# A decoder trunk on one core: 1/rms multiplied into the results of the up products instead of their operands

## The chip, the cores and the metric

The kernel runs on one core of one Trainium2 chip. The metric is the device time of one execution in microseconds (us). The profile tells the engines apart as PE (TensorE matmul), PEld (TensorE weight load), DVE (VectorE), ACT (ScalarE), POOL (GpSimd) and SP (SyncE, which here issues the transfers).

## The reference

One inference step of a two-layer trunk on 1024 prompt tokens and 8 x 4 sample tokens (1056 columns in the kernel, D = 1024). Layer 0 is a gated linear recurrence, layer 1 a dilated window attention. Each ends with the same MLP of width 4096, and the change is about that:

```python
def _rmsnorm(x, gain):
    return x * lax.rsqrt(jnp.mean(x * x, axis=-1, keepdims=True) + EPS) * gain

def _sqrelu_mlp(x, w_up, w_down):
    return jnp.square(jax.nn.relu(x @ w_up)) @ w_down

x = x + h
x = x + _sqrelu_mlp(_rmsnorm(x, mlp_norm[layer]), mlp_w_up[layer], mlp_w_down[layer])
```

## The kernel before, in words

All activations are kept transposed: 128 feature rows by token columns, eight row blocks `xr[:, k, :]`. In the MLPs and in the output products ahead of them the 1056 columns are cut in three chunks, 384, 384 and 288 (`MLPCH`). Every large fp32 product is made of three matmuls of rounded halves: high by high, low by high and high by low (`mm3`, L185 to L187, and `mmx`, L805 to L807). So every operand is split in two: ACT copies it into the rounded type (the H half), and another engine subtracts that copy from it (the L half).

**Weights.** `_prep` loads a weight in two transfers (`wraw`, issued on SP), splits it (`whi` on ACT, L131; `wlo` on POOL, L132), and for a down weight `w_dn` also makes four sums (L159 to L161 on DVE, L162 on POOL) and splits these into `whix` (ACT) and `wlox` (POOL). The sums belong to a scheme in the manner of Strassen, by which four products of 2 x 2 blocks are made with seven. The raw tiles lie in two buffers, so a transfer can start only when POOL has finished the `wlo` of the tile that it replaces.

**Norm.** `norm` (L254) runs as a lane, a generator that is advanced one step between products. Per chunk it squares each row block (ACT, L263 and L266), adds the squares up (DVE, L267) and sums over the 128 rows with one matmul against a constant matrix (PE, L273). ACT then makes 1/rms by logarithm and exponential (L239, L240). For each row block DVE multiplies x by gain and 1/rms (L281), ACT copies the high half (L232), and POOL (five of eight) or DVE (three) subtracts for the low half (L233).

**MLP.** `mlp` takes the 32 hidden blocks in eight groups of four. For a group it makes the up product j = 0, then four down products (`down`) of the group before, and then the up products j = 1 to 3. An up product has 24 matmuls per chunk and leaves a PSUM tile `pj`, of which there are four. `ev_up` empties it: ACT takes the relu out of PSUM (L720), DVE squares it (L721), and the result, or differences of results (L726, L743), is split (ACT L709; L710 on DVE or POOL). `down` works on PSUM tiles A, B and C; DVE adds each partial result to the residual (`add`, L819), and the next product into the same tile waits for that add. The third chunk goes through `alone` and `resid` (L211).

The order of instructions on each engine comes from a scheduler that goes by program order and priorities (`high_priority`). Each engine then runs its own instructions strictly in that order.

Of the kernel before, what the change touches and what calls it, by code (L numbers as in the profile page):

```python
# [10 lines left out]
F32 = mybir.dt.float32  # L11
F32R = mybir.dt.float32r
U8 = mybir.dt.uint8
AF = mybir.ActivationFunctionType
# [4 lines left out]
P = 128  # L19
KD = 8  # L20
# [26 lines left out]
class Kern:  # L47
# [202 lines left out]
    def norm(self, gi, ops, need, gaps=(3, 3, 2), hp=0):  # L250
# [3 lines left out]
        for c, sl in enumerate(self.chunks_of(ops)):  # L254
# [16 lines left out]
            with self.tc.high_priority(offset=hp):  # L271
# [3 lines left out]
                for k in range(KD):  # L275
# [5 lines left out]
                        nc.vector.scalar_tensor_tensor(t, xk, self.gains[:, gi, k:k + 1], r, op0=ALU.mult, op1=ALU.mult)  # L281
                    self.split(c, k, ops, t, pool=(k % 3 != 0))

    def chunks_of(self, ops):
        return CHUNKS if ops[0][0].shape[-1] == CW else MLPCH


    def phase_a(self):
# [140 lines left out]
        part(range(4, 8))  # L429
        ctx.close()  # L430
        self.open_norm()
        self.lanes.append(self.norm(G_M0, ops, NEED, (3, 3, 0), 100))
        ctx = ExitStack()
        self.wx = ctx.enter_context(tc.tile_pool(name="wxA", bufs=4, reuse_waits="tile"))
        self.rawx = True
# [264 lines left out]
    def mlp(self, layer, ops, after=None):  # L700
# [11 lines left out]
        def ev_up(hs, hb, j, tmp, last):  # L712
# [3 lines left out]
            def ev(c, ps):  # L716
                n = ps.shape[-1]
                with tc.high_priority(offset=200):
                    r = self.tmp(n)
                    nc.scalar.activation(r, ps, AF.Relu)  # L720
                nc.vector.tensor_tensor(r, r, r, op=ALU.mult)  # L721
                if c == 2:
                    return split(hs[2 * e + i], r, True)
                tmp[e, c] = r

                sub = lambda x, y: nc.vector.tensor_tensor(x, y, x, op=ALU.subtract)  # L726
                h = hb[i]
                if c == 0:
                    split(h[e], r, True)
                elif last:  # L730
                    split(h[2 + e], r)
                elif e == 0:
                    t = tmp[0, 0]
                    sub(t, r)
                    split(h[3], t)
                else:
                    split(h[2], r)
                    t2, t3, t4 = tmp[0, 0], tmp[0, 1], tmp[1, 0]
                    sub(t3, r)
                    split(h[5], t3)  # L740
                    sub(t2, r)
                    split(h[4], t2)
                    nc.vector.tensor_tensor(t4, t4, t2, op=ALU.subtract)  # L743
                    split(h[6], t4)
# [30 lines left out]
        for g in range(NG + 1):  # L775
# [9 lines left out]
                        self.down(2 * p, self.wnext(), hs, hb)  # L785
            if g < NG:
                ups(g, range(1, GS))
        w = [self.wnext() for _ in range(4)]
        if after:
            self.lanes.append(self.norm(None, after, NEED))  # L790
# [69 lines left out]
    def phase_c(self, ops):  # L860
# [51 lines left out]
        while not self.merged:  # L912
            self.tick()
        w = [self.wnext() for _ in range(4)]
        self.lanes.append(self.norm(G_M1, ops, NEED))
        for c, sl in enumerate(MLPCH):
            while self.merged < -(-min(sl.stop, NP_ + P) // P) * 2 - (c == 2):
                next(self.queue[0])
            for m, t, ks in self.quarter_items(w, 4):
# [1 line left out]
                self.mm3(ps, t, ops[c], ks)  # L921
                self.resid(m, c, ps)
                self.tick()
        self.drain()
        cxa.close()
        self.open_norm()
        return ops
# [542 lines left out]
```

## Time and profile before

| | |
|---|---|
| time, median of 3 runs (lowest, highest) | 3043.11 us (3035.6, 3047.07) |
| time of the profiled execution | 3045.13 us |
| its span, from first to last instruction | 3043.4 us |
| mean granted TensorE clock | 0.989 |
| busy PE, PEld | 2875.0 (94%), 2757.8 us (91%) |
| busy DVE, ACT, POOL | 1796.0 (59%), 1282.9 (42%), 1338.3 us (44%) |

The busy share says how long an engine worked, not whether anyone waited for it. The MLPs take the stretches from about 765 to 1440 us and 2320 to 2990 us of the span; the stretches from 660 and from 2262 us are the output products ahead of them, with the norm that they overlap. A row of the timeline gives start and duration of an operation and, in brackets, how long the engine had stood idle before it and what released it. PEclk is the share of full TensorE speed that the chip granted.

### The profile page before, as it was taken

The page shows a single profiled execution, that of the slowest core. Times are in us where ns is not written, and L with a number is a line of the kernel's source. Part 1 is how long each engine was busy: PE and PEld are TensorE (multiplying, and loading weights), DVE is VectorE, ACT ScalarE, POOL GpSimd, SP SyncE. Part 2 cuts the span into 40 slices and gives each one's busy share as a digit, 9 for nine tenths or more (in the row PEclk, how much of TensorE's full clock was granted, in tenths as well). Part 3 has the DMA queues.
Part 4 walks back from the last instruction along what each step waited for, and adds up shares of the span by engine and source line. Part 5 has one row for each costly group of instructions (what it writes and reads, how often), then busy time and mean ns, then how long its engine had stood idle before and what let it go on. Part 6 is the DMA issues. An engine that isn't in the chain of part 4 may idle for free.

```text
span 3043.4 us, 47407 instructions
## 1 busy us (share of the span) xinstructions
PE 2875.0 (94%) x18144; PEld 2757.8 (91%) x18144; DVE 1796.0 (59%) x3467; ACT 1282.9 (42%) x2972; POOL 1338.3 (44%) x1149
## 2 busy tenths in 40 slices
PE   6998999889999999999899999999999999999999
PEld 5888888889999999999899889889888999999999
DVE  8777777876544455543654565665676455544442
ACT  6555656643332222332445544555544223332221
POOL 5444444453544444544463553333225445444442
PEclk9999999999999999999999999999999999999999
DMA  3100211230111111112212233332641111111112
GB/s 113 36 30 30 71 40 29 69 123 18 46 49 43 49 46 46 49 43 63 84 62 68 84 99 108 124 117 71 195 150 42 44 48 49 42 46 46 49 49 86
DMA packets 131956, 201.92 MB, mean 66 GB/s; under 512 B 26320, under 2 KB 65872, under 8 KB 129680
## 3 DMA queue, kind: packets, MB, share of 16 engines
q1 hardware_dynamic: 131728, 198.88, 20.9%
q8 instruction: 143, 2.34, 0.3%
q14 instruction: 85, 0.70, 0.1%
HBM read 164.04 MB, written 34.80 MB: 65 GB/s over the span
## 4 chain that ended last, share of the span: by engine, by line
PE 56%; DVE 10%; POOL 8%; issue 7%; DMA 5%; ACT 3%; POOLq 0%; SPq 0%; DVEq 0%; ACTq 0%
PE pj L185 10%; PE pj L186 10%; PE pj L187 10%; POOL wlo L132 4%; PE pj L805 4%; PE pj L806 4%; PE pj L807 4%; DMA wraw<-w_dn 3%; PE g L806 2%; PE g L805 2%; PE g L807 2%; POOL wlox L132 2%; PE g L1143 2%; PE g L1115 1%; PE g L1130 1%
## 5 line engine op out<-in xcount | busy, mean ns | idle before, releaser
L185 PE MATMUL pj<-opH,whi 128*128 128x352 f32 (+2 forms) x3408 | 1136.7, 334 | 9.9 <-DVE xr L211 3.5
L186 PE MATMUL pj<-opL,whi 128*128 128x352 f32 (+2 forms) x3408 | 1110.1, 326 | 5.0 <-POOL opL L233 3.2
L187 PE MATMUL pj<-opH,wlo 128*128 128x352 f32 (+2 forms) x3408 | 1107.0, 325 | 2.9 <-POOL wlo L132 2.7
L132 POOL TENSOR_TENSOR wlo<-wraw,whi 128x512 fp32r<-128x512 f32 x404 | 546.5, 1371 | 913.1 <-ACT whi L131 882.1
L185 PEld LDWEIGHTS pj<-opH,whi 128*128 128x128 f32 x3408 | 645.8, 190 | 30.6 <-issue 16.9
L186 PEld LDWEIGHTS pj<-opL,whi 128*128 128x128 f32 x3408 | 646.7, 190 | 17.9 <-POOL opL L233 6.6
L187 PEld LDWEIGHTS pj<-opH,wlo 128*128 128x128 f32 x3408 | 645.6, 189 | 6.9 <-POOL wlo L132 4.1
L131 ACT ACTIVATE whi<-wraw 128x512 fp32r<-128x512 f32 x404 | 232.6, 621 | 546.6 <-PE g L806 439.9
L721 DVE TENSOR_TENSOR tmp<-tmp 128x384 f32<-128x384 f32 (+1 forms) x192 | 169.5, 883 | 311.2 <-ACT tmp L720 311.2
L819 DVE TENSOR_TENSOR xr<-xr,pj 128x384 f32<-128x384 f32 x336 | 183.7, 553 | 138.5 <-PE pj L807 138.3
L496 POOL TENSOR_TENSOR lv<-b 128x512 f32<-128x512 f32 x112 | 125.0, 1127 | 102.7 <-PE g L593 58.4
L720 ACT ACTIVATE tmp<-pj 128x384 f32<-128x384 f32 (+1 forms) x192 | 86.9, 453 | 189.3 <-PE pj L187 188.5
L132 POOL TENSOR_TENSOR wlox<-wsum,whix 128x512 fp32r<-128x512 f32 x112 | 151.0, 1368 | 0.6 <-ACT whix L131 0.6
L162 POOL TENSOR_TENSOR wsum<-wraw,wsum 128x256 f32<-128x256 f32 x56 | 43.7, 781 | 168.0 <-DVE wsum L160 153.8
L1117 DVE CUSTOM_DVE_ANT_0 pr<-g,band,rq 128x128 f32<-128x128 f32 (+1 forms) x192 | 67.9, 405 | 79.9 <-PE g L1115 76.3
L1120 ACT ACTIVATE pr<-pr,nm 128x128 f32<-128x128 f32 (+1 forms) x192 | 84.1, 440 | 68.0 <-DVE nm L1118 67.8
L148 POOL TENSOR_TENSOR wraw<-wraw,gains 128x512 f32<-128x512 f32 x72 | 91.4, 1275 | 40.0 <-DMA wraw<-w_q 33.3
L211 DVE TENSOR_TENSOR xr<-xr,pj 128x384 f32<-128x384 f32 (+1 forms) x132 | 67.2, 516 | 69.7 <-PE pj L187 37.5
L709 ACT ACTIVATE hbH<-tmp 128x384 fp32r<-128x384 f32 x106 | 54.9, 526 | 121.2 <-DVE tmp L721 72.8
L967 POOL TENSOR_TENSOR q<-q,cos 32x512 f32<-32x512 f32 x48 | 89.8, 1877 | 30.2 <-DVE rsw L966 28.9
L159 DVE TENSOR_TENSOR wsum<-wraw 128x256 f32<-128x256 f32 x56 | 23.8, 425 | 131.5 <-DMA wraw<-w_dn 131.3
L806 PE MATMUL g<-hL,whi 128*128 128x288 f32 x336 | 100.5, 299 | 0.0
(399 smaller groups left out, 5917.8 us busy)
## 6 DMA issues: line engine op xcount, KB each, us to landing
wraw<-w_up SPq DMA_DIRECT2D x128, 256.0 KB, 2.8
wraw<-w_dn SPq DMA_DIRECT2D x128, 256.0 KB, 2.8
wraw<-w_in SPq DMA_DIRECT2D x64, 256.0 KB, 2.8
wraw<-w_q SPq DMA_DIRECT2D x48, 256.0 KB, 2.9
ub<-us SPq DMA_DIRECT2D x32, 256.0 KB, 2.2
cc<-ck SPq DMA_DIRECT2D x8, 1024.0 KB, 5.1
cc<-cv SPq DMA_DIRECT2D x8, 1024.0 KB, 5.4
wraw<-w_kv SPq DMA_DIRECT2D x24, 256.0 KB, 2.9
```

Source lines behind the costliest of these rows:

```text
L131: nc.scalar.activation(hi[:, j:j + 4, :], raw, AF.Copy)
L132: nc.gpsimd.tensor_tensor(lo[:, j:j + 4, :], raw, hi[:, j:j + 4, :].bitcast(F32), op=ALU.subtract)
L148: nc.gpsimd.tensor_tensor(raw, raw, self.gains[:, gi, j:j + 4][:, :, None].to_broadcast([P, 4, P]), op=ALU.mult)
L185: nc.tensor.matmul(ps, wh[:, kw, :], xh[:, kx, :], start=(i == 0), stop=False)
L186: nc.tensor.matmul(ps, wh[:, kw, :], xl[:, kx, :], start=False, stop=False)
L187: nc.tensor.matmul(ps, wl[:, kw, :], xh[:, kx, :], start=False, stop=(i == len(ks) - 1))
L496: nc.gpsimd.tensor_tensor(r(lv), r(b), r(b)[:, :, h - 1:h].to_broadcast([P, 256 // h, 2 * h]), op=ALU.subtract)
L721: nc.vector.tensor_tensor(r, r, r, op=ALU.mult)
L805: nc.tensor.matmul(ps, wh[:, kw, :], xh, start=start and i == 0, stop=False, skip_group_check=True)
L806: nc.tensor.matmul(ps, wh[:, kw, :], xl, start=False, stop=False, skip_group_check=True)
L807: nc.tensor.matmul(ps, wl[:, kw, :], xh, start=False, stop=stop and i == len(items) - 1, skip_group_check=True)
L819: self.nc.vector.tensor_tensor(x(i, c), x(i, c), ps, op=ALU.add)
```

## The change

`norm_late` takes the place of `norm` in the two MLPs. Its operands are the split of x times gain, without 1/rms: ACT makes the high half in one operation, DVE the low half (multiply and subtract in one), and POOL none. 1/rms goes to tiles of its own, one per chunk (`scale`, with a number behind the name in the order of instructions). `ev_up` multiplies it in: DVE takes the maximum with zero and multiplies by the scale, straight from PSUM, and ACT squares. The entry of the second MLP no longer runs all lanes to their end before it goes on.

```diff
--- before.py
+++ after.py
@@ -280,6 +280,44 @@
                     else:
                         nc.vector.scalar_tensor_tensor(t, xk, self.gains[:, gi, k:k + 1], r, op0=ALU.mult, op1=ALU.mult)
                     self.split(c, k, ops, t, pool=(k % 3 != 0))
+
+    def open_scales(self):
+
+        self.sctx = ExitStack()
+        p = self.sctx.enter_context(self.tc.tile_pool(name=f"sc{self.wi}", bufs=1, side="right", reuse_waits="tile"))
+        self.scale = [p.tile([P, sl.stop - sl.start], F32, name=f"scale{c}") for c, sl in enumerate(MLPCH)]
+
+    def norm_late(self, gi, ops, need, gaps=(3, 3, 2), hp=0):
+
+        nc = self.nc
+        steps = 0
+        for c, sl in enumerate(MLPCH):
+            n, r = sl.stop - sl.start, self.scale[c]
+            for k in range(KD):
+                while steps < need[c] - (KD - 1 - k):
+                    yield
+                    steps += 1
+                with self.tc.high_priority(offset=hp):
+                    if k == 0:
+                        nc.scalar.activation(r, self.xr[:, 0, sl], AF.Square)
+                    else:
+                        t = self.sq(n)
+                        nc.scalar.activation(t, self.xr[:, k, sl], AF.Square)
+                        nc.vector.tensor_tensor(r, r, t, op=ALU.add)
+            with self.tc.high_priority(offset=hp + 60):
+                for k in range(KD):
+                    h, l = (t[:, k, :] for t in ops[c])
+                    x, g = self.xr[:, k, sl], self.gains[:, gi, k:k + 1]
+                    nc.scalar.activation(h, x, AF.Copy, scale=g)
+                    nc.vector.scalar_tensor_tensor(l, x, g, h.bitcast(F32), op0=ALU.mult, op1=ALU.subtract)
+            for _ in range(gaps[c]):
+                yield
+                steps += 1
+            with self.tc.high_priority(offset=hp):
+                ps = self.bank()[:, :n]
+                nc.tensor.matmul(ps, self.onesD, r, start=True, stop=True)
+                nc.scalar.activation(r, ps, AF.Ln, bias=self.eps[:, 0:1])
+                nc.scalar.activation(r, r, AF.Exp, scale=-0.5)
 
     def chunks_of(self, ops):
         return CHUNKS if ops[0][0].shape[-1] == CW else MLPCH
@@ -429,7 +467,9 @@
         part(range(4, 8))
         ctx.close()
         self.open_norm()
-        self.lanes.append(self.norm(G_M0, ops, NEED, (3, 3, 0), 100))
+        self.open_scales()
+        self.lanes.append(self.norm_late(G_M0, ops, NEED, hp=100))
+        next(self.lanes[-1])
         ctx = ExitStack()
         self.wx = ctx.enter_context(tc.tile_pool(name="wxA", bufs=4, reuse_waits="tile"))
         self.rawx = True
@@ -717,8 +757,8 @@
                 n = ps.shape[-1]
                 with tc.high_priority(offset=200):
                     r = self.tmp(n)
-                    nc.scalar.activation(r, ps, AF.Relu)
-                nc.vector.tensor_tensor(r, r, r, op=ALU.mult)
+                    nc.vector.scalar_tensor_tensor(r, ps, 0.0, self.scale[c], op0=ALU.max, op1=ALU.mult)
+                nc.scalar.activation(r, r, AF.Square)
                 if c == 2:
                     return split(hs[2 * e + i], r, True)
                 tmp[e, c] = r
@@ -785,6 +825,7 @@
                         self.down(2 * p, self.wnext(), hs, hb)
             if g < NG:
                 ups(g, range(1, GS))
+        self.sctx.close()
         w = [self.wnext() for _ in range(4)]
         if after:
             self.lanes.append(self.norm(None, after, NEED))
@@ -912,7 +953,9 @@
         while not self.merged:
             self.tick()
         w = [self.wnext() for _ in range(4)]
-        self.lanes.append(self.norm(G_M1, ops, NEED))
+        self.open_scales()
+        self.lanes.append(self.norm_late(G_M1, ops, NEED))
+        next(self.lanes[-1])
         for c, sl in enumerate(MLPCH):
             while self.merged < -(-min(sl.stop, NP_ + P) // P) * 2 - (c == 2):
                 next(self.queue[0])
@@ -921,7 +964,9 @@
                 self.mm3(ps, t, ops[c], ks)
                 self.resid(m, c, ps)
                 self.tick()
-        self.drain()
+        while self.queue:
+            if next(self.queue[0], "end") == "end":
+                self.queue.popleft()
         cxa.close()
         self.open_norm()
         return ops
```

The order of instructions moves with it. On DVE, around the first down product of a group (a middle group of the first MLP; `pj` and `g` are PSUM tiles, `xr` the residual, `wsum` the sums of the down weight, `hpL` the low half of a hidden block), the row before reads

```order
L159 TENSOR_TENSOR wsum<-wraw 128x256
L721 TENSOR_TENSOR tmp<-tmp 128x384
L160 TENSOR_TENSOR wsum<-wsum,wraw 128x256
L161 TENSOR_TENSOR wsum<-wraw 128x256
L721 TENSOR_TENSOR tmp<-tmp 128x384
L726 TENSOR_TENSOR tmp<-tmp 128x384
L710 TENSOR_TENSOR hpL<-tmp,hpH 128x384
L819 TENSOR_TENSOR xr<-xr,pj 128x384
L721 TENSOR_TENSOR tmp<-tmp 128x288
L819 TENSOR_TENSOR xr<-xr,g 128x384
L819 TENSOR_TENSOR xr<-xr,pj 128x384 x2
```

and now

```order
L760 SCALAR_TENSOR_TENSOR tmp<-pj,scale_6842 128x384
L159 TENSOR_TENSOR wsum<-wraw 128x256
L161 TENSOR_TENSOR wsum<-wraw 128x256
L160 TENSOR_TENSOR wsum<-wsum,wraw 128x256
L760 SCALAR_TENSOR_TENSOR tmp<-pj,scale_6843 128x384
L766 TENSOR_TENSOR tmp<-tmp 128x384
L750 TENSOR_TENSOR hpL<-tmp,hpH 128x384
L760 SCALAR_TENSOR_TENSOR tmp<-pj,scale_6844 128x288
L860 TENSOR_TENSOR xr<-xr,pj 128x384
L860 TENSOR_TENSOR xr<-xr,g 128x384
L860 TENSOR_TENSOR xr<-xr,pj 128x384 x2
```

The squares that stood on DVE (L721) are gone from the row; in their places stand the new operations that read PSUM (L760). The one of the third chunk (288 columns), which stood behind the first add, now stands ahead of it, and the second chunk's weight sums (L160, L161) no longer wait behind the first chunk's square.

On ACT, at the same place (`whix` and `whi` are the weights' high halves, `hpH` and `h0H` those of hidden blocks), before:

```order
L720 ACTIVATE tmp<-pj 128x384
L709 ACTIVATE hpH<-tmp 128x384
L131 ACTIVATE whix<-wsum 128x512 x2
L720 ACTIVATE tmp<-pj 128x384
L709 ACTIVATE hpH<-tmp 128x384
L131 ACTIVATE whi<-wraw 128x512 x2
L720 ACTIVATE tmp<-pj 128x288
L709 ACTIVATE h0H<-tmp 128x288
```

and now:

```order
L761 ACTIVATE tmp<-tmp 128x384
L749 ACTIVATE hpH<-tmp 128x384
L131 ACTIVATE whix<-wsum 128x512 x2
L761 ACTIVATE tmp<-tmp 128x384
L749 ACTIVATE hpH<-tmp 128x384
L131 ACTIVATE whi<-wraw 128x512 x2
L761 ACTIVATE tmp<-tmp 128x288
L749 ACTIVATE h0H<-tmp 128x288
```

Every relu (L720) has become a square (L761) at the same place in the row; it reads a tile that DVE wrote instead of PSUM.

On DVE at the entry of the second MLP, where the third chunk's squares are summed for the last norm matmul (`us` before, a `scale` tile now; `pt` is a working tile), before:

```order
L281 SCALAR_TENSOR_TENSOR pt<-xr,gains,rstd 128x384 x3
L267 TENSOR_TENSOR us<-us,pt 128x288
L211 TENSOR_TENSOR xr<-xr,pj 128x288 x3
L267 TENSOR_TENSOR us<-us,pt 128x288
L233 TENSOR_TENSOR opL<-pt,opH 128x384
L267 TENSOR_TENSOR us<-us,pt 128x288 x5
L281 SCALAR_TENSOR_TENSOR pt<-xr,gains,rstd 128x288 x3
```

and now:

```order
L211 TENSOR_TENSOR xr<-xr,pj 128x288
L312 SCALAR_TENSOR_TENSOR opL<-xr,gains,opH 128x288 x2
L211 TENSOR_TENSOR xr<-xr,pj 128x288
L312 SCALAR_TENSOR_TENSOR opL<-xr,gains,opH 128x288 x2
L306 TENSOR_TENSOR scale_21786<-scale_21786,pt 128x288 x2
L760 SCALAR_TENSOR_TENSOR tmp<-pj,scale_21784 128x384
L760 SCALAR_TENSOR_TENSOR tmp<-pj,scale_21785 128x384
```

Before, the second chunk's last scale operations (L281) and five of the seven sums (L267) stood in a block around the last residual adds (L211). Now the third chunk's own scale operations (L312) stand there, and only two sums are left behind the last residual add. On PE the matmul that uses the sum moves 17 matmuls down the row, to just ahead of the third chunk of the first up product.

## Rows read from the trace of the kernel before

**Rows 1.** Busy time by window (start:end, length; PE, PEld, DVE, ACT, POOL; PEclk; DMA; GB/s).

```profile
660.00:765.00 105.00, 101.60 (x605) 97.63 (x604) 63.66 (x99) 41.66 (x87) 42.45 (x34) 1.00 0.17 55
...
765.00:1440.00 675.00, 655.95 (x4051) 652.00 (x4050) 328.68 (x554) 201.90 (x402) 313.77 (x266) 0.99 0.16 48
...
2262.00:2320.00 58.00, 50.85 (x296) 47.80 (x296) 47.12 (x82) 29.79 (x66) 26.02 (x22) 0.94 0.09 29
...
2320.00:2990.00 670.00, 652.57 (x4030) 648.93 (x4030) 329.98 (x556) 200.69 (x399) 311.08 (x264) 0.99 0.15 47
...
906.00:910.00 4.00, 3.52 (x11) 3.53 (x12) 1.34 (x3) 1.15 (x2) 3.41 (x3) 0.58 0.30 91
...
2306.00:2310.00 4.00, 4.00 (x14) 3.79 (x13) 2.13 (x5) 2.25 (x5) 0.63 (x1) 0.56 0.00 0
```

**Rows 2.** Waits of PE, whole program (us in total, times, longest).

```profile
PE pj L805 <- DVE xr L819: 36.5, 26, 1.9
```

**Rows 3.** Timeline of PE (start, us, what, [idle before <- releaser]).

```profile
992.19 0.45 PE L805 MATMUL pj<-hqH,whix 128*128 128x384 f32 x1 [1.68 <-DVE xr L819]
...
999.93 0.44 PE L805 MATMUL pj<-hqH,whix 128*128 128x384 f32 x1 [1.16 <-DVE xr L819]
```

**Rows 4.** Timeline of DVE, 980 to 1002 us.

```profile
984.50 0.55 DVE L721 TENSOR_TENSOR tmp<-tmp 128x384 f32<-128x384 f32 x1
...
985.30 0.42 DVE L161 TENSOR_TENSOR wsum<-wraw 128x256 f32<-128x256 f32 x1
...
987.39 1.56 DVE L721 TENSOR_TENSOR tmp<-tmp 128x384 f32<-128x384 f32 x1 [1.67 <-ACT tmp L720]
...
989.06 1.46 DVE L726 TENSOR_TENSOR tmp<-tmp 128x384 f32<-128x384 f32 x1
...
991.11 0.56 DVE L710 TENSOR_TENSOR hpL<-tmp,hpH 128x384 fp32r<-128x384 f32 x1 [0.59 <-ACT hpH L709]
...
991.59 0.55 DVE L819 TENSOR_TENSOR xr<-xr,pj 128x384 f32<-128x384 f32 x1
...
997.48 0.43 DVE L159 TENSOR_TENSOR wsum<-wraw 128x256 f32<-128x256 f32 x1 [2.81 <-DMA wraw<-w_dn]
...
998.86 1.01 DVE L819 TENSOR_TENSOR xr<-xr,pj 128x384 f32<-128x384 f32 x2
```

**Rows 5.** Timeline of ACT, the same stretch.

```profile
986.35 0.64 ACT L131 ACTIVATE whix<-wsum 128x512 fp32r<-128x512 f32 x1 [0.22 <-POOL wsum L162]
...
986.89 0.47 ACT L720 ACTIVATE tmp<-pj 128x384 f32<-128x384 f32 x1
...
990.56 0.52 ACT L709 ACTIVATE hpH<-tmp 128x384 fp32r<-128x384 f32 x1 [3.20 <-DVE tmp L726]
...
990.99 1.13 ACT L131 ACTIVATE whi<-wraw 128x512 fp32r<-128x512 f32 x2
```

**Rows 6.** Timeline of POOL, the same stretch.

```profile
987.26 2.85 POOL L132 TENSOR_TENSOR wlox<-wsum,whix 128x512 fp32r<-128x512 f32 x2
...
991.68 2.76 POOL L132 TENSOR_TENSOR wlo<-wraw,whi 128x512 fp32r<-128x512 f32 x2 [1.57 <-ACT whi L131]
```

**Rows 7.** Chain of waits, 955 to 1003 us (start, us, what).

```profile
978.59 2.97 POOL wlo L132 x2
...
981.57 2.49 DMA wraw<-w_dn
```

**Rows 8.** Groups of one shape, DVE (count | busy us, mean ns | idle before).

```profile
L819 DVE TENSOR_TENSOR xr<-xr,pj 128x384 f32<-128x384 f32 x336 | 183.7, 553 | 138.5 <-PE pj L807 138.3
...
L993 DVE SCALAR_TENSOR_TENSOR kt<-pj,hg,rstd 128x352 f32<-128x352 f32 x12 | 9.1, 760 | 18.5 <-ACT rstd L240 18.5
...
L281 DVE SCALAR_TENSOR_TENSOR tmp<-xr,gains,rstd 128x384 f32<-128x384 f32 x16 | 16.4, 1071 | 0.4 <-ACT rstd L240 0.4
```

**Rows 9.** Waits of PE at the entries: 700 to 765, then 2275 to 2320 us.

```profile
PE pj L185 <- DVE xr L211: 2.5, 1, 2.5
...
PE g L273 <- DVE us L267: 4.1, 2, 3.7
```

## The prediction

> **What bounds the kernel now.** I read five views: the busy table with its windows by stage, the waits of TensorE, the timelines of the vector engines around one wait, the chain of waits, and the groups of instructions by shape. TensorE (PE) is busy in 2875.0 of 3043.4 us, so what can be won is the time in which it stands still, or runs at the lower clock. The change touches only the two MLPs and their entries. There PE is busy 655.95 of 675 us and 652.57 of 670 us in the steady part, and 101.60 of 105 and 50.85 of 58 us at the entries [rows 1]. It does not remove a matmul, so the whole prize is bounded by the idle time of these four windows, 19.05 + 17.43 + 3.40 + 7.15 = 47.0 us, and the time lost to a lower granted clock in them.
>
> In the steady part there is one wait only: the first matmul of a down product waits for the add that empties its PSUM tile, 26 times, 36.5 us in all [rows 2]. That is the idle time of the two steady windows, 19.05 + 17.43, to the last tenth, 13 waits in each. The waits come in pairs, two per group of four hidden blocks; the pair at 992.19 (1.68 us) and 999.93 (1.16 us) [rows 3] is the usual one.
>
> Why is the add late? Read the four vector queues together. PE finished the tile long before, but the add (991.59) stands in VectorE's (DVE) queue behind work for the next group's first up product: a square (987.39, 1.56 us), a difference (989.06, 1.46 us), and a subtraction (991.11, 0.56 us) that itself waited for ScalarE's (ACT) copy [rows 4, 5]. That sequence starts when ACT is through with whix (986.35 + 0.64 = 986.99) and reads the relu out of PSUM. Durations add up without a gap: 0.47 relu + 1.56 square + 1.46 difference + 0.52 copy + 0.56 subtraction + 0.55 add = 5.12, from 986.99 to 992.11; the add ended at 992.14. The second wait is the same lateness passed on through the weights: the copy's end (990.99) lets whi start, then GpSimd's (POOL) wlo (991.68, 2.76 us), then the next weight's transfer, which lands before DVE's wsum at 997.48, which stands ahead of the adds at 998.86 [rows 4 to 6]. The square and the difference take 1.46 to 1.56 us because POOL's wlox runs from 987.26 to 990.11 [rows 6]; the same operation took 0.55 us at 984.50, before POOL began.
>
> **The change part by part.**
>
> *Evacuation of the up products.* Relu on ACT and square on DVE become a maximum-and-scale on DVE that reads PSUM, and a square on ACT. On the path of the first wait this takes out 0.47 + 1.56 us and puts in ACT's square. ACT's operations on 384 columns take 0.47 to 0.52 us [rows 5]; I take 0.53. The new DVE operation on the second chunk runs before the path starts: DVE is through with wsum at 985.30 + 0.42 = 985.72 [rows 4], and whix holds ACT until 986.99. The order also moves the third chunk's evacuation (288 columns) ahead of the first add, which adds its duration. So the new path is 0.53 + 1.46 + 0.52 + 0.56 + 0.45 + 0.55 = 4.07, which is 1.05 less: the add ends at 991.06 and the wait falls from 1.68 to 0.63.
>
> The trace does not show this DVE operation on this shape. The nearest rows are the add that reads one operand from PSUM, 0.553 us over 336 of them, and a scale-and-multiply out of PSUM, 0.760 us over 12 [rows 8]; the upper bound is the contended square, 1.56 us. I take the add's figure (0.45 for 288 columns), since the adds hold 0.55 us in a stretch in which POOL is busy half of the time. By the upper bound the 288-column one costs some 1.2 and the gain on the first wait falls from 1.05 to 0.3.
>
> The Trainium skill, "SBUF — State Buffer", section "SBUF: two separate sides", says that a DVE operation with two SBUF inputs and a GpSimd operation lock each other out for a whole instruction. By it the new evacuation, with one input in PSUM, would never be held up (0.45), while the difference with two SBUF inputs stays at 1.46; the trace agrees so far, 1.56 for the square against 0.55 for the adds. Against the change speaks the same skill's "VectorE: DVE Perf Modes", section "Specifications": ScalarE sits closer to PSUM and VectorE closer to SBUF, so that PSUM reads belong on ACT. By the rows the loss is 0.553 against 0.47, under 0.1 us per instruction, at most 0.2 us per wait.
>
> Two things follow from the same edit. First, the copy ends 0.47 + 1.56 - 0.53 = 1.50 us sooner, so whi, wlo, the transfer and wsum come 1.50 sooner while PE comes 1.05 sooner: the second wait falls by 0.45 to 0.71. Second, the same square also stands in the path one up product earlier, where wlo (978.59, to 981.56) holds the transfer (981.57) that starts all of the above [rows 7]. If that too comes about 1.1 us sooner, the first wait is gone (PE 1.68 sooner), the weights are 2.6 sooner, and the second wait is 1.16 - 0.92 = 0.24. Per pair this makes a gain of 1.50 in the first case and 2.60 in the second, for 13 pairs 19.5 or 33.8 us. Nothing shows which holds for all groups; I take the middle, **27 us**.
>
> *Clock.* After the longest waits the granted clock falls from 1.00 to 0.58 or 0.56 for some 4 us, [rows 1] at 906 and 2306. Its price is 3.52 x 0.42 = 1.5 us and 4.00 x 0.44 = 1.8 us. The steady windows show 0.99 for 1.00 elsewhere, which is 0 to 6.6 us each. [...] I take **2 us** of gain for both MLPs together; bounds 0 and 7.
>
> *Entry of the first MLP.* The operands no longer need 1/rms: eight scale operations of two SBUF inputs remain per chunk, but the subtractions go, five of eight of them on POOL and three on DVE. Before, PE waited 2.5 us for a residual add [rows 9] that stood behind DVE's eight scale operations, of 1.071 us each [rows 8], and three subtractions, some 10.5 us together; in the new order seven such operations stand ahead of that add, 7.5 us. The 3 us less are more than the wait, so it goes, and of the other 0.9 us of the window most goes with POOL's subtractions: **3 us** (bounds 0 and 3.4, the window's idle time).
>
> *Entry of the second MLP.* The matmul that sums the third chunk's squares stood ahead of the first up product and waited 3.7 of 4.1 us [rows 9]; it moves 17 matmuls on, to just ahead of the third chunk, which is 17 x 652.57 / 4030 = 2.8 us [rows 1], and on DVE the second chunk's scale operations now stand before the last residual adds, not among them. So the whole 3.7 goes. The clock stretch at 2306 follows that wait and goes with it (1.8 us). Of the other 3.05 us idle, mostly waits for residual adds, I take 2.5. So **8 us**; bounds 3 and 7.15 + 3.05 (50.85 x 0.06 of clock) = 10.2. What hides the late scale now is the up product itself; if the scale came after its end, PSUM buffers would hold PE for the difference.
>
> *No cost.* ACT's squares and copies stay in number; ACT is busy 202 of 675 us. In the steady part DVE and POOL carry as many instructions as before. The transfers' order does not change.
>
> **Sum.** 27 + 2 + 3 + 8 = 40 us off the profiled execution, which took 3045.13 us with a span of 3043.4: 3005. The three runs have a median of 3043.11, 2 us lower, far inside their spread of 11 us, so I leave it at 3005. Its own range is 2994 (33.8 + 4 + 3.4 + 10) to 3018 (19.5 + 0 + 2 + 5.5).
>
> **The rivals.**
> (a) *The chain is only re-dealt.* The new order still has whix ahead of ACT's square, the difference beside wlox and now the third chunk's evacuation ahead of the add. If the evacuations are held up by POOL (1.56 and 1.2 us), the gain on the steady waits shrinks to 0.3 per first wait, 4 us in all, and only the entries gain 11: 3030. For it: every DVE operation with SBUF operands is stretched in this stretch. Against: the 336 adds are not.
> (b) *All of it goes.* Both waits vanish in all groups with their clock stretches: 36.5 + 7 + 3 + 9 = 56, or 2989. For it: the middle of the first wait's cases is near zero. Against: the weights' chain (wlo 2.8, transfer 3.0, wsum) stays as long as it was.
> (c) *Slower.* DVE, not ACT, now opens the chain: the second chunk's evacuation cannot start until wsum is done at 985.72 and takes 1.56, so ACT's square ends at 987.81, the difference at 989.27, the copy at 989.79; a subtraction stretched to 1.5 and 1.2 for the third chunk put the add's end at 993.04, 0.9 later than now. Then the first wait is 2.6 us, and each would bring the lower clock: 13 x (0.9 + 1.5) = 31, less 11 at the entries: 3065. It decides from the point where the evacuations of 384 columns take over about 1.3 us on average.
> (d) *A case between:* the first wait alone shrinks, by 1.05, and the second stays, because the weights' chain is held by a transfer and not by whi: 13.6 + 11 = 25, or 3020.
>
> **How the numbers follow.** Forecast 0.50, (b) 0.15, (d) 0.15, (a) 0.13, (c) 0.07. A change of 0.5% (15 us, about what a measurement of this kernel can tell from none) puts the line at 3028 to 3030: the forecast, (b), and most of (d) are faster, (a) is mostly within. That gives 0.78 faster, 0.15 same, 0.07 slower. The range for 8 in 10 runs from 2986, a little below (b), to 3032, which takes in (d) and most of (a).
>
> **What would show it.** The wait of the down product's first matmul for the add should fall from 36.5 us in 26 to about 10 us, with the second of a pair the larger one. The new DVE evacuation should last about 0.55 us for 384 columns, the differences still about 1.5 beside POOL, and the wait for the sum of squares at 2305 should be gone. I am wrong if the evacuation shows means near 1 us, if the first adds wait for the third chunk's evacuation, or if a transfer, and not DVE's queue, ends the remaining waits.

## The result, and the profile after

The changed kernel takes 2988.02 us in the median of four runs (2987.43 to 2996.47), the kernel before 3045.09 us beside it. The ratio is 0.9822, with a 95% interval of 0.9806 to 0.9839: 57 us less, where 40 were forecast. The time lies in the predicted range (2986 to 3032), near its lower end, and at the figure of rival (b), 2989, though not by its mechanism. The profiled execution has a span of 2985.6 us for 3043.4. One of all the executions below, of the run sbuf_evac, was slow (4857.78 us at a mean granted clock of 0.666), and its ratio leaves that one out.

Where the time went can be read by following the same matmul in both traces. Both have 18,144 matmuls in nearly the same order; the table gives the time between the starts of numbers 4000, 4280, 8400, 11000, 13460, 13800 and 17750, worked out from the two traces. The stretches that it leaves out (up to 4000, 8400 to 11000, behind 17750) differ by less than 1 us each.

| stretch (matmul numbers) | before, us | after, us | difference | forecast |
|---|---|---|---|---|
| entry of the first MLP (4000 to 4280) | 48.1 | 42.5 | -5.6 | -3 |
| first MLP (4280 to 8400) | 687.1 | 669.1 | -18.0 | -29 for both MLPs |
| attention, ahead of the second entry (11000 to 13460) | 389.5 | 381.0 | -8.5 | 0 |
| entry of the second MLP (13460 to 13800) | 66.2 | 55.8 | -10.4 | -8 |
| second MLP (13800 to 17750) | 657.2 | 641.4 | -15.8 | (above) |

The waits of PE for the add, over the whole program of the changed kernel (total, times, longest):

```profile
PE pj L846 <- DVE xr L860: 9.7, 16, 1.3
```

That is 9.7 us in 16 for 36.5 in 26 [rows 2], 26.8 us less; the forecast had 27. The windows of the first MLP's entry, of its steady part, 58 us around the second entry (the same piece of work lies some 41 us earlier now) and the second steady part show a granted clock of 1.00 (columns as in [rows 1]):

```profile
660.00:765.00 105.00, 104.87 (x640) 103.26 (x639) 50.80 (x96) 45.56 (x94) 28.41 (x22) 1.00 0.17 57
765.00:1440.00 675.00, 670.25 (x4150) 666.77 (x4150) 310.12 (x570) 212.32 (x409) 315.06 (x268) 1.00 0.17 50
2221.00:2279.00 58.00, 57.27 (x355) 55.58 (x355) 44.16 (x100) 34.22 (x79) 10.05 (x8) 1.00 0.18 57
...
2279.00:2929.00 650.00, 644.86 (x4006) 641.76 (x4005) 300.16 (x553) 204.74 (x394) 307.77 (x260) 1.00 0.16 47
```

Compare the counts with [rows 1]: 640 matmuls for 605 in the first window, 4150 for 4051 in the second. The waits for the residual add at 733 us and for the third chunk's sum at 2305 us [rows 9] have no row left.

The pair of waits in the same group as before. On PE only the second is left (985.34, for 999.93 in [rows 3]):

```profile
985.34 0.44 PE L846 MATMUL pj<-hqH,whix 128*128 128x384 f32 x1 [0.57 <-DVE xr L860]
```

DVE around it; [rows 4] are the rows to lay beside these:

```profile
968.66 0.54 DVE L760 SCALAR_TENSOR_TENSOR tmp<-pj,scale 128x384 f32<-128x384 f32 x1
...
971.77 0.42 DVE L160 TENSOR_TENSOR wsum<-wsum,wraw 128x256 f32<-128x256 f32 x1
972.11 0.55 DVE L760 SCALAR_TENSOR_TENSOR tmp<-pj,scale 128x384 f32<-128x384 f32 x1
974.25 1.46 DVE L766 TENSOR_TENSOR tmp<-tmp 128x384 f32<-128x384 f32 x1 [1.59 <-ACT tmp L761]
976.30 0.98 DVE L750 TENSOR_TENSOR hpL<-tmp,hpH 128x384 fp32r<-128x384 f32 x1 [0.59 <-ACT hpH L749]
977.21 0.45 DVE L760 SCALAR_TENSOR_TENSOR tmp<-pj,scale 128x288 f32<-128x288 f32 x1
977.57 0.54 DVE L860 TENSOR_TENSOR xr<-xr,pj 128x384 f32<-128x384 f32 x1
...
982.89 0.43 DVE L159 TENSOR_TENSOR wsum<-wraw 128x256 f32<-128x256 f32 x1 [2.80 <-DMA wraw<-w_dn]
...
984.27 1.01 DVE L860 TENSOR_TENSOR xr<-xr,pj 128x384 f32<-128x384 f32 x2
```

ACT and POOL in the same stretch, for [rows 5] and [rows 6]:

```profile
973.10 0.63 ACT L131 ACTIVATE whix<-wsum 128x512 fp32r<-128x512 f32 x1 [0.24 <-POOL wsum L162]
973.64 0.51 ACT L761 ACTIVATE tmp<-tmp 128x384 f32<-128x384 f32 x1
975.74 0.53 ACT L749 ACTIVATE hpH<-tmp 128x384 fp32r<-128x384 f32 x1 [1.60 <-DVE tmp L766]
976.17 1.14 ACT L131 ACTIVATE whi<-wraw 128x512 fp32r<-128x512 f32 x2
```

```profile
974.00 2.87 POOL L132 TENSOR_TENSOR wlox<-wsum,whix 128x512 fp32r<-128x512 f32 x2
976.86 2.82 POOL L132 TENSOR_TENSOR wlo<-wraw,whi 128x512 fp32r<-128x512 f32 x2
```

The path has the order that the prediction gave it: evacuation (972.11) ready before whix is through (973.10 + 0.63 = 973.73), then the square (0.51), the difference (1.46, beside wlox), the copy (0.53), the subtraction (0.98, where 0.56 was put, since it now begins at 976.30, while the second half of wlox runs to 976.87), the third chunk's evacuation (0.45) and the add (0.54), which ends at 978.11. From the end of whix that is 4.38 us; 4.07 were forecast, and before it was 5.15 (a sum of durations of 5.12). PE does not wait for this add any more. Taken from the first matmul of the down product (987.23 before, 974.86 now, in the traces), the add ends after 3.25 us where it ended after 4.91: 1.66 us sooner, just the wait of 1.68. About half, 0.89, is that whix ends sooner (1.13 us ahead of that matmul for 0.24), the rest, 0.77, that the path is shorter. The second wait of the pair is left because the transfer starts when wlo has ended (976.86 + 2.82) and wsum (982.89) stands ahead of the adds. The chain of waits gives the transfer:

```profile
976.86 2.83 POOL wlo L132 x2
...
979.71 3.09 DMA wraw<-w_dn
```

By shape, on DVE (count, then busy us, mean ns, idle before):

```profile
L766 DVE TENSOR_TENSOR tmp<-tmp 128x384 f32<-128x384 f32 x84 | 80.7, 987 | 47.4 <-ACT tmp L761 47.4
...
L760 DVE SCALAR_TENSOR_TENSOR tmp<-pj,scale 128x384 f32<-128x384 f32 x128 | 71.2, 556 | 293.6 <-PE pj L187 293.6
```

The new evacuation takes 0.556 us, like the add (0.553), and not the 0.760 or 1.56 of the bounds [rows 4, 8]. Of its 128 executions on 384 columns 43 began while a POOL operation was running, and none of them took more than 0.560 us.

At the second entry DVE finishes the third chunk's sums at 2264.66 + 2.11 = 2266.77, and PE comes to the matmul only at 2270.4:

```profile
2263.84 0.89 DVE L312 SCALAR_TENSOR_TENSOR opL<-xr,gains,opH 128x288 fp32r<-128x288 f32 x1 [0.58 <-ACT opH L311]
2264.66 2.11 DVE L306 TENSOR_TENSOR scale<-scale,pt 128x288 f32<-128x288 f32 x2
```

### The profile page after: what moved, and what is told of

Read it like the earlier page. It is cut to its first block, busy times and chain, and to the rows that moved or that the text cites. A ratio compares the mean times of both kernels' runs of the same rounds, so it can differ in the third digit from the quotient of the medians.

```text
span 2985.6 us, 47235 instructions
## 1 busy us (share of the span) xinstructions
PE 2859.0 (96%) x18144; PEld 2747.8 (92%) x18144; DVE 1710.1 (57%) x3449; ACT 1296.0 (43%) x2972; POOL 1301.6 (44%) x1119
## 4 chain that ended last, share of the span: by engine, by line
PE 55%; DVE 10%; POOL 10%; DMA 6%; issue 6%; ACT 3%; SPq 0%; POOLq 0%; DVEq 0%; ACTq 0%
PE pj L185 10%; PE pj L186 10%; PE pj L187 10%; POOL wlo L132 5%; DMA wraw<-w_dn 4%; PE pj L846 4%; PE pj L847 4%; PE pj L848 4%; POOL wlox L132 2%; PE g L847 2%; PE g L846 2%; PE g L848 2%; PE g L1188 2%; PE g L1160 1%; PE g L1175 1%
## 5 line engine op out<-in xcount | busy, mean ns | idle before, releaser
L760 DVE SCALAR_TENSOR_TENSOR tmp<-pj,scale 128x384 f32<-128x384 f32 (+1 forms) x192 | 100.0, 521 | 301.6 <-PE pj L187 301.6
L761 ACT ACTIVATE tmp<-tmp 128x384 f32<-128x384 f32 (+1 forms) x192 | 94.7, 493 | 290.1 <-DVE tmp L760 290.0
L211 DVE TENSOR_TENSOR xr<-xr,pj 128x384 f32<-128x384 f32 (+1 forms) x132 | 67.7, 517 | 77.2 <-PE pj L187 39.0
L766 DVE TENSOR_TENSOR tmp<-tmp 128x384 f32<-128x384 f32 x84 | 80.7, 987 | 47.4 <-ACT tmp L761 47.4
L846 PE MATMUL g<-hH,whi 128*128 128x288 f32 x336 | 98.9, 294 | 0.0
```

Source lines behind the costliest of these rows:

```text
L760: nc.vector.scalar_tensor_tensor(r, ps, 0.0, self.scale[c], op0=ALU.max, op1=ALU.mult)
L761: nc.scalar.activation(r, r, AF.Square)
L846: nc.tensor.matmul(ps, wh[:, kw, :], xh, start=start and i == 0, stop=False, skip_group_check=True)
```

## The experiments

Each kernel was compared with the kernel before on the same chip. Stretches are those of the table above. "E1" and "E2" are the two entries, "MLPs" the two steady stretches together (1344.3 us before, 1310.5 after).

| run | median, us | ratio to before (95%) | E1 | MLPs | attention | E2 | waits for the add |
|---|---|---|---|---|---|---|---|
| evac_only | 3008.50 | 0.9888 (0.9873 to 0.9903) | 48.0 | 1310.2 | 383.5 | 67.3 | 9.8 in 17 |
| both_on_act | 3008.62 | 0.9886 (0.9871 to 0.9901) | 49.6 | 1311.8 | 381.3 | 66.2 | 13.2 in 16 |
| late_only | 3029.79 | 0.9946 (0.9926 to 0.9965) | 42.5 | 1342.7 | 390.7 | 55.6 | 35.2 in 25 |
| sbuf_evac | 3024.86 | 0.9934 (0.9915 to 0.9954) | 42.5 | 1340.0 | 386.3 | 55.6 | 36.5 in 28 |
| with_drain | 2996.33 | 0.9838 (0.9821 to 0.9855) | 42.5 | 1312.0 | 384.0 | 57.2 | 10.9 in 18 |
| raw3 | 2975.87 | 0.9773 (0.9758 to 0.9787) | 42.5 | 1300.2 | 376.6 | 55.6 | 0.8 in 2 |
| before_raw3 | 3003.41 | 0.9865 (0.9850 to 0.9880) | 49.9 | 1306.9 | 379.3 | 66.7 | 5.1 in 12 |
| before_again | 3038.64 (one run) | | 49.4 | 1344.1 | 384.1 | 66.6 | |
| after_again | 2990.92 (one run) | | 42.5 | 1311.1 | 379.9 | 55.5 | |

**One half of the change alone: the evacuation.** The tile of ones is made once, at the start; the diff leaves that out.

```diff
 (kernel before)
-                    nc.scalar.activation(r, ps, AF.Relu)
-                nc.vector.tensor_tensor(r, r, r, op=ALU.mult)
+                    nc.vector.scalar_tensor_tensor(r, ps, 0.0, self.ones[:, :n], op0=ALU.max, op1=ALU.mult)
+                nc.scalar.activation(r, r, AF.Square)
```

> The kernel before (operands still carry 1/rms, entries as before) with only the evacuation of the up products changed: DVE takes the maximum out of PSUM and multiplies by a tile of ones, ACT squares. Theory: the gain inside the MLPs comes from this edit alone. The waits of the down product for the add fall from 36.5 us in 26 to about 10 in 16, and the time falls by 33 to 35 us, to about 3010; the waits at the entries (2.5 us at 733, 3.7 us at 2305) stay. Rival: the late scale and the other order at the entries are what makes the MLPs faster (they set how far the weights are ahead); then this is within 8 us of before, 3037 to 3045, with the 36.5 us of waits.

The MLPs take 1310.2 us, as in the changed kernel, and the waits at the entries are still there:

```profile
PE pj L807 <- DVE xr L821: 9.8, 17, 1.3
...
PE pj L187 <- DVE xr L213: 4.9, 3, 2.5
...
PE g L275 <- DVE us L269: 4.1, 2, 3.7
```

So the steady gain, 34 us, is that of the evacuation, and none of it of the late scale.

**The square moved, the reading of PSUM not.**

```diff
 (kernel before)
                     nc.scalar.activation(r, ps, AF.Relu)
-                nc.vector.tensor_tensor(r, r, r, op=ALU.mult)
+                nc.scalar.activation(r, r, AF.Square)
```

> The kernel before with the relu left on ACT, reading PSUM, and only the square moved from DVE to ACT. Theory: what counts is that no square with SBUF operands stands on DVE beside POOL's wlox; the path of the first wait is 0.47 + 0.53 + 1.46 + 0.52 + 0.56 + 0.55 = 4.09 for 5.12, the third chunk's work is off DVE altogether, so the waits fall to 10 to 15 us and the time by 28 to 35 us, to 3010 to 3017. Rival: it is DVE's reading of PSUM ahead of the weights' sums that does it; then ACT, still behind whix with two operations, keeps most of the waits, 25 us or more, and the time is 3030 or more.

The MLPs gain 32.5 us, the waits are 13.2 us. Whether ACT or DVE empties PSUM hardly counts (1311.8 and 1310.2 us); that DVE no longer squares an SBUF tile in this row does.

**The other half alone: the late scale.** This kernel leaves out the multiplication by 1/rms, so it computes something else; only its times are used.

```diff
 (changed kernel)
-                    nc.vector.scalar_tensor_tensor(r, ps, 0.0, self.scale[c], op0=ALU.max, op1=ALU.mult)
-                nc.scalar.activation(r, r, AF.Square)
+                    nc.scalar.activation(r, ps, AF.Relu)
+                nc.vector.tensor_tensor(r, r, r, op=ALU.mult)
```

> The changed kernel with the old evacuation (relu on ACT, square on DVE); the multiplication of the up results by 1/rms is left out. Theory: only the entries gain. The 36.5 us of waits in 26 come back; at the entries the waits at 733 and 2305 stay gone; the time is that of before less 14 to 17 us (5.6 at the first entry, 10 at the second), 3028 to 3031, and less another 8 (3021) if the shorter stretch ahead of the second entry belongs to the change too. Rival: the steady waits fall here too (under 25 us), which gives 3015 or less.

```profile
PE pj L846 <- DVE xr L860: 35.2, 25, 1.9
```

Both entries are as short as in the changed kernel and the MLPs as long as before but for 1.6 us, no more than one stretch varies between two executions (up to 1.9 us, below). The two halves nearly add up: 34.1 and 1.6 us in the MLPs, 5.6 and 10.6 at the entries for the second half alone, where the change itself has 33.8 and 16.0.

**The evacuation with its operand in SBUF.**

```diff
 (changed kernel)
-                    nc.vector.scalar_tensor_tensor(r, ps, 0.0, self.scale[c], op0=ALU.max, op1=ALU.mult)
+                    nc.scalar.activation(r, ps, AF.Relu)
+                nc.vector.scalar_tensor_tensor(r, r, 0.0, self.scale[c], op0=ALU.max, op1=ALU.mult)
                 nc.scalar.activation(r, r, AF.Square)
```

> The changed kernel with one step more: ACT takes the relu out of PSUM, DVE multiplies that SBUF tile by the scale, ACT squares. Theory: the DVE operation, with two operands in SBUF, is held up beside POOL and takes about 1.5 us where it took 0.556, and it stands behind whix again: the path is 0.47 + 1.5 + 0.53 + 1.46 + 0.52 + 0.56 + 0.8 + 0.55 = 6.4, 1.3 more than before; the waits are 45 to 65 us and the time 3030 to 3055. Rival: the place of the operand does not matter and the operation takes about 0.6; then the path is some 5.1 and the waits stay below 36 us, the time below 3025.

The theory does not fit, and the rival comes close: the waits are back (36.5 us in 28, where it had less than 36), the median is 3024.86 (less than 3025), and in the group shown below the path from the end of whix (984.48 in the trace) to the end of the add (989.58) is the 5.1 us that it gave. The MLPs are as long as 1340.0 us, so the step more costs nearly the whole steady gain, all but 4.3 us. But it does not do it by the 1.5 us that I gave the operation on 384 columns:

```profile
L761 DVE SCALAR_TENSOR_TENSOR tmp<-tmp,scale 128x384 f32<-128x384 f32 x128 | 79.1, 618 | 262.5 <-ACT tmp L760 262.4
L761 DVE SCALAR_TENSOR_TENSOR tmp<-tmp,scale 128x288 f32<-128x288 f32 x64 | 75.1, 1174 | 32.2 <-ACT tmp L760 32.2
```

It took 0.618 us in the mean (0.558 in the median, over 0.7 in 18 of 128); the one on 288 columns was stretched, to 1.174 in the mean. The order on POOL had shifted with the edit: the second chunk's operation now began at the end of the first half of wlox, just ahead of POOL's next operation, and it was that one that took longer:

```profile
984.88 0.56 DVE L761 SCALAR_TENSOR_TENSOR tmp<-tmp,scale 128x384 f32<-128x384 f32 x1 [1.75 <-ACT tmp L760]
986.34 1.63 DVE L767 TENSOR_TENSOR tmp<-tmp 128x384 f32<-128x384 f32 x1 [0.91 <-POOL hpL L750]
```

```profile
983.69 1.30 POOL L132 TENSOR_TENSOR wlox<-wsum,whix 128x512 fp32r<-128x512 f32 x1
984.95 1.35 POOL L750 TENSOR_TENSOR hpL<-tmp,hpH 128x384 fp32r<-128x384 f32 x1
986.27 1.28 POOL L132 TENSOR_TENSOR wlox<-wsum,whix 128x512 fp32r<-128x512 f32 x1
```

POOL's subtraction of 384 columns at 984.95 lasts 1.35 us, where the 16 of that form in the kernel before took 1.01 in the mean; DVE's difference at 986.34, behind it, 1.63. In this run 28 of the 64 subtractions of that form on POOL took 1.35 to 1.38 us, in the kernel before none more than 1.03. The difference itself had to wait 0.91 us for that subtraction. In these rows the operation that begins first keeps its time and the other one is stretched, so a mean price for "beside POOL" cannot be carried from one order to another; the last section has the price of a single one.

**The second entry with the lanes run to their end.**

```diff
 (changed kernel)
-        while self.queue:
-            if next(self.queue[0], "end") == "end":
-                self.queue.popleft()
+        self.drain()
```

> The changed kernel, but the entry of the second MLP again runs all lanes to their end before it goes on. Only the matmul that sums the third chunk's squares moves, 29 matmuls up the row; DVE's order is that of the changed kernel. Theory: the second entry gained because DVE has less to do ahead of these sums, not because of the matmul's place. In the changed kernel the sums end at 2266.8 and PE is at the matmul's new place at 2265.5, so it waits 1.3 us and loses some 1.5: 2989 to 2990, no measurable change. Rival: the place of the matmul is the gain; then the wait is 3.5 us or more with a stretch of lower clock behind it, 5 us or more in the stretch of the second entry.

```profile
PE g L318 <- DVE scale L306: 1.5, 1, 1.5
```

The wait is 1.5 us and the second entry 57.2 us, 1.4 more than in the changed kernel, as the theory had it. The median, 2996.33, is above the 2989 to 2990 expected and 8 us above the changed kernel's of another session; 3.0 us of the profiled execution's lie in the attention stretch and 1.5 in the MLPs, which this edit does not touch. The two ratios to the kernel before, 0.9838 (0.9821 to 0.9855) and 0.9822 (0.9806 to 0.9839), do not differ clear of the noise.

**A third buffer for the raw weights, in the changed kernel and in the kernel before.**

```diff
-    raw = (self.wx if x is True and self.rawx else self.wp).tile([P, 4, P], F32, name="wraw")
+    raw = (...).tile([P, 4, P], F32, name="wraw", **({} if x is True and self.rawx else dict(bufs=3)))
```

> The changed kernel with a third buffer for the raw weight tiles, so that a transfer does not wait for POOL's wlo of the tile before the last. Theory: what is left of the waits (9.7 us in 16) is the weights' chain, wlo, transfer, wsum, ahead of the adds; the transfer comes some 3 us sooner and the waits go, below 3 us; 10 to 13 us less, 2975 to 2978. Rival: the weights' sums are not what holds the adds, or something else of the chain (POOL) takes its place: 7 us of waits or more and 2984 or more.

> The kernel before with the third raw buffer and nothing else. Theory: the first waits come from the DVE square and difference beside POOL and stay in part, the second ones from the weights' chain and go; 36.5 us of waits fall to 10 to 22, the time by 15 to 30 us, to 3013 to 3028. Rival: all of it is the weights' chain (the path starts when whix is through, and whix waits for a transfer); then the waits fall below 5 us and the time by 35 us or more. Second rival: the transfers are not late, and nothing changes, 3038 to 3045.

```profile
PE pj L846 <- DVE xr L860: 0.8, 2, 0.6
```

```profile
PE pj L805 <- DVE xr L819: 5.1, 12, 0.6
```

The first row is that of raw3, the second that of before_raw3. In the changed kernel the rest of the waits goes, 9.7 to 0.8 us, and the time falls to 2975.87 us, the best of all. It shows that the second wait was the weights' chain. In the kernel before, the buffer alone does what the evacuation does, and a little more: 5.1 us of waits are left, and 1306.9 us of the MLPs for 1310.5. That is more than the theory allowed (10 us of waits or more) and nearly the first rival (below 5). Its rows show why. DVE and ACT in the same group:

```profile
976.11 0.96 DVE L159 TENSOR_TENSOR wsum<-wraw 128x256 f32<-128x256 f32 x1 [0.22 <-DMA wraw<-w_dn]
...
980.30 1.42 DVE L721 TENSOR_TENSOR tmp<-tmp 128x384 f32<-128x384 f32 x1 [2.08 <-ACT tmp L720]
...
983.79 0.56 DVE L710 TENSOR_TENSOR hpL<-tmp,hpH 128x384 fp32r<-128x384 f32 x1 [0.59 <-ACT hpH L709]
984.26 0.55 DVE L819 TENSOR_TENSOR xr<-xr,pj 128x384 f32<-128x384 f32 x1
```

```profile
978.84 0.63 ACT L131 ACTIVATE whix<-wsum 128x512 fp32r<-128x512 f32 x1 [0.43 <-POOL wsum L162]
...
979.79 0.47 ACT L720 ACTIVATE tmp<-pj 128x384 f32<-128x384 f32 x1
983.23 0.53 ACT L709 ACTIVATE hpH<-tmp 128x384 fp32r<-128x384 f32 x1 [2.97 <-DVE tmp L726]
```

The square is stretched as before (1.42 us), and from the start of the relu (979.79) to the end of the add (984.26 + 0.55 = 984.81) there are 5.02 us, where there were 5.25 (986.89 to 992.14 in [rows 4, 5]). But PE does not wait for this add. From the first matmul of the down product (982.36 here), wsum starts 6.25 us ahead, where it started 3.07 ahead in the kernel before (984.16 to 987.23), whix ends 2.89 ahead for 0.24, and the add ends 2.45 after for 4.91. The path is nearly as long as ever; it starts in time.

**Both kernels once more.**

> The kernel before once more, unchanged, for a second profile. Open is why the attention stretch ahead of the second entry was 8.5 us shorter in the changed kernel, from 289.5 to 281.0 us, though nothing in it is changed. Theory: the waits there for the cache transfers vary from one execution to the next; then this stretch differs from 289.5 by 3 us or more, while the MLP stretches repeat within 1 us (687 and 657). Rival: it belongs to the change, and this stretch repeats within 1.5 us.

> The changed kernel once more, unchanged, for a second profile. Theory: the attention stretch differs from 281.0 us by 3 us or more, while the MLP stretches repeat within 1 us (669 and 641). Rival: it repeats within 1.5 us, and the 8.5 us belong to the change.

The two lengths of the attention stretch are misprinted in these texts by 100 us: it took 389.5 and 381.0. A second execution of the kernel before took 384.1 there, of the changed one 379.9. The MLPs repeat within 1.9 us per stretch, not within the 1 us expected. So 5 us of this stretch come and go with the execution in the one kernel and 1 us in the other. Over all profiles, the four whose MLPs are long have 384.1 to 390.7, the seven others 376.6 to 384.0.

## Why the prediction was right, and where its numbers were off

*Waits of the down products.* Forecast 27 us of 36.5, measured 26.8. The first wait of a pair is gone and the second left at about 0.6 us, as the second of the two cases put it (0 and 0.24); the middle (of 19.5 and 33.8 us) was taken for want of evidence, so that it hit to 0.2 us is luck. The residue of 0.57 us is larger than 0.24 because the weights come 2.22 us sooner, and not 2.60 (counted from the first matmul of the down product, wsum starts after 8.03 us, where it started after 10.25): wlo, which now follows wlox at once, starts 2.45 us sooner, and it and the transfer together take 0.23 us longer. One of the signs of being wrong did show: what ends the remaining waits is a transfer (wsum at 982.89 had waited 2.80 us for it, and raw3, where transfers start sooner, takes 8.9 of the 9.7 us away). The prediction has that chain in its account of the second wait, so the account stands, but the sign as it was put speaks against it.

*What the path was made of.* The prediction gave the first wait to the length of the path (1.05 of 1.68 us) and only then to its late start. In the changed kernel the two have about equal parts, 0.77 and 0.89 us. An earlier start is also enough by itself: before_raw3 leaves the length as it was and removes most of the waits. That DVE, and not ACT, now reads PSUM was no part of the cause (both_on_act).

*Clock.* This term was mis-sized; the two kernels' traces do not show its 2 us. The MLPs lost 33.8 us, 26.8 of them waits; the other 7.0 stood as 2 in the sum, with 7 as the bound. The granted clock of the steady windows rose from 0.99 to 1.00, and the traces show that this is nearly all of it. In the kernel before PE ran four times for 3.4 us at half clock (0.50, the level of 1.2 GHz) in the steady MLPs, from 906.7, 1084.2, 2459.7 and 2736.2 us, each time right behind a wait of 1.77 to 1.94 us; another wait of 1.93 us, at 1176.7, had no such stretch behind it. Two of them (columns as in [rows 1]):

```profile
906.70:910.10 3.40, 3.40 (x12) 3.40 (x12) 0.64 (x2) 1.15 (x2) 2.81 (x3) 0.50 0.39 119
...
2459.70:2463.10 3.40, 3.40 (x14) 3.40 (x14) 2.30 (x4) 0.44 (x1) 2.72 (x3) 0.51 0.37 96
```

The changed kernel has none there. Half of 4 x 3.4 us is 6.8 us, so the upper bound was the better figure for this pair; the second execution of the kernel before lost 8.5 us in this way, late_only 6.8 and sbuf_evac 1.7, with much the same waits. The sum closes in all eleven profiles: without PE's waits and half of the time at half clock the MLPs last 1298.6 to 1301.9 us in every one of them, so little is left for any other cost of a wait.

*Entries.* Mis-sized too, 16.0 for 11. The first took 5.6 us off where its window held only 3.40 us of idle time, which I had set as the bound. PE's idle time was the wrong measure: its busy share in that window was 101.60 of 105 us, but it made 605 matmuls there, and now 640 [rows 1]; 35 matmuls at 104.87 / 640 are 5.7 us. The bound should have been taken from the count, or from the weight loads (PEld), whose busy time rose by the full 5.63 us, from 97.63 to 103.26. In the trace before, the matmul that waited for the residual add started 2.79 us after the one ahead of it, and seven others that needed a low half from POOL or DVE started 0.28 to 0.61 us after theirs, where now there are 0.13 to 0.18; that is another 1.9 us, of which the profile counts 0.6 as waits. The second gave 10.4 us, just over its bound of 10.2: PE's waits fell from 7.1 to 0.7 us, and the 6.8 us at half clock from 2302.7 on are gone. The wait for the sum went too, and with_drain shows that it is mainly the new norm's shorter row on DVE that did it: with the matmul ahead of the first up product again (number 13721 on PE; 13732 before, 13750 in the changed kernel) it waits 1.5 us and not 3.7.

*Attention.* Forecast 0, measured 8.5. This part is open. The same kernel varies by 5.4 us there, so no single figure can be given to the change; the means of the two groups of profiles lie some 7 us apart. What the difference is made of can be read: PE's waits in the stretch are 21.4 us before and 15.4 after, about half of the difference (3.0 us) for transfers of the cache, and 13.7 us at half clock became 6.8. Without the waits and half of that time the stretch lasts 361.3 to 362.9 us in all eleven profiles. Why the waits vary is not shown; the orders on SP and POOL are the same in both_on_act (381.3 us) as in the kernel before. Without these 8.5 us the time would be some 2996, still in the range, and nearer to the forecast.

*The rivals.* (a) and (c) needed an evacuation held up by POOL, over 1 us; it took 0.556. What was said for (a), that every DVE operation with SBUF operands is stretched in that stretch, goes too far: the subtraction at 991.11 took 0.56 us, while POOL stood idle from 990.11 to 991.68 [rows 4, 6]. (b) came out at the same time, 2989, by waits that all vanish, together with the clock and the entries; it was right on the clock (7), but 9.7 us of the waits stayed, and the entries and the attention made up for it. (d), that the second wait stays as it was, did not hold; that it is the weights' chain, which (d) named, did (raw3).

## What to carry to other kernels

Where an engine waits for an operation that is short by itself, write down the whole row ahead of it with both its length and what lets it start; here either a shorter path or an earlier start removed the same waits, and the earlier start (one more buffer of 2 KB per partition) was the cheaper. Two remedies for one wait do not add: 34 and 37 us alone, 44 together in the MLPs. To bound what a stretch can give, count its matmuls against the same count elsewhere, or take the busy time of the weight loads; the busy time of the matmuls hid part of a stall here (3.4 us idle, 5.6 us won).

## What was not expected of the hardware

A DVE operation with two SBUF inputs was held up beside POOL in one order (1.56 us) and not in another (0.56), where POOL's operation was stretched instead (1.35 for 1.01 us). The single instructions show a rule. In the kernel before, 92 operations of this kind (DVE, two SBUF inputs, 384 columns; lines L710, L721, L726 and L743) began while a POOL operation had more than 0.1 us to run: each ended 0.41 to 0.43 us after that POOL operation, so it took up to 1.66 us. In the 28 during which POOL began one, and the 268 others, none took more than 0.56 us; in the 28 it is POOL's wlo that is held up, to some 1.15 us after DVE's end. In the changed kernel 98 of 112 were held up in the same way; the other 14, all begun within 0.05 us of POOL's wlo, kept their 0.55 us, and wlo took 1.74 us. In the rows of sbuf_evac above, wlox ends at 986.27 + 1.28 = 987.55 and the difference at 986.34 + 1.63 = 987.97. Operations of DVE with one input in PSUM were not held up at all: 225 of the adds of the kernel before began while POOL was running, and none took more than 0.557 us.

The mean of a shape hides this. The evacuations of sbuf_evac, all 192 of both shapes (min, median, max in ns), have a median near their least and a largest almost three times that:

```profile
L761 DVE SCALAR_TENSOR_TENSOR tmp<-tmp,scale x192: 549/559/1551, 746.0 to 2979.1; 128x384 f32<-128x384 f32 x128, 128x288 f32<-128x288 f32 x64
```

So an operation beside POOL is priced by the single instructions in its stretch (here the rest of POOL's operation and 0.41 us for 384 columns), not by its group.
